# Attention scores of two heads on the two halves of the array's rows, with new tables of order and places, in a hybrid decoder layer

## The chip, the cores and the metric

The kernel runs on one core of a Trainium2 chip. The metric is the device time of one execution in microseconds; the time of a kernel is the median of its runs.

## The reference

One decoder layer for 512 tokens of width 1024, batch 1, float32 throughout. The input is normalised and multiplied by one wide matrix; its columns are the queries, keys and values of three attentions and three gates. The attentions are a sliding-window attention (8 query heads, 2 key heads of width 64, window 128, with a sink and a bias by distance), a stick-breaking attention (8 heads of width 64) and a cross-attention to 256 memory rows (4 heads of width 128). Each branch is projected, gated and added, then come an output matrix, a residual, and a SwiGLU network of width 2816.

```python
# sliding window, blocks of 128 queries against this block and the one before
scores = einsum('bnqhgd,bnkhd->bnhgqk', qb, kband) * d ** -0.5 + bias     # d = 64
# stick-breaking, block i of queries against all keys up to it
z = einsum('bqhd,bkhd->bhqk', q[:, i * 128:L], k[:, :L]) * d ** -0.5      # d = 64
log_1m = where(causal, log_sigmoid(-z), 0)
between = cumsum(log_1m, reverse) - log_1m
a = where(causal, exp(log_sigmoid(z) + between), 0)
out = einsum('bhqk,bkhd->bqhd', a, v[:, :L])
```

## The kernel before

**Precision.** A float32 factor x is kept as two parts in the type float32r: `hi`, a copy rounded on ScalarE, and `lo` = x - hi on VectorE (`split`, line 423). A product of two such factors is three matmuls into the same PSUM bank, hi*hi, hi*lo and lo*hi (`mm3`, line 455). Transposes and the products with the attention weights are in plain float32; one such matmul instruction appears in the trace as two passes.

**Units.** Most of the work is a stream of units (`Stream`, line 307): load a weight tile, split it, do its matmuls. `dn.run(us)` issues pieces of the stream worth that many microseconds by the units' own estimates. The attentions (`sb_head`, `swa_pair`, `mem_pair`) are issued between such pieces.

**Scores before.** A head is 64 wide, and the two heads of a pair lie on partitions 0-63 and 64-127 of one tile of 128 x 512. To fill the 128 rows of the array, `proj` (line 581) hands a finished block to one of two helpers, both of which work head by head on 64 partitions:

- `stack_parts` (line 553, for the stick-breaking keys `kb` and the sliding-window queries `qa`) puts hi on the head's own 64 partitions and lo on the other 64: one ScalarE copy and one VectorE subtraction a head.
- `stack_twice` (line 564, for the queries `qb` and the keys `ka`) puts hi on both halves, and lo on the head's half with zeros on the other: a GpSimd fill, a ScalarE copy, a VectorE subtraction and a VectorE copy a head.

There are 13 such blocks: four each of `kb`, `qb` and `qa`, and one `ka`. A head's score block is then two matmuls over all 128 rows: (hi, lo) against (hi, hi), and hi against lo with zeros. In `sb_head` (line 1273) a head has four query blocks with 512, 384, 256 and (two copies of 128, to fill the bank) 256 key columns, into three PSUM banks. In `swa_pair` (line 1348) a head has four query blocks of 256 columns each, into two banks.

**Around the scores.** After the scores of a head, ScalarE reads each bank twice (two sigmoids, into `br` and `bw`), VectorE masks and scans, `sb_turn` (line 1306) transposes the weights on TensorE (`c_ident`, `bw` in the trace), and `sb_out` (line 1323) multiplies them with the values: two heads on the two halves of the array's columns, 64 stationary columns each (`at`, `wide` in the trace, with the form 128x64). `swa_pair` ends in the same way (`pts`, `wide`). There are four calls of each.

**Order and places.** `ORDER` (line 38) holds one list for each engine: the order in which its instructions stand, counted as the program issues them; `Noted` (line 220) records them, and the end of the program (line 2095) chains them with dependencies that carry no semaphore. `PLAN` (line 148) names, for each buffer that is asked for, which place of its kind it gets: 8 PSUM banks, 73 tiles of 128 x 512 and others. Since every instruction goes through the recorder, nearly all lines of the trace are line 232.

Of the kernel before, what the change touches and what calls it, by code (L numbers as in the profile page):

```python
# [17 lines left out]
P = 128  # L18
# [19 lines left out]
ORDER = {  # L38
    "tensor": (
# [23 lines left out]
    ),  # L63
    "vector": (
# [81 lines left out]
    ),  # L146
}
PLAN = {
    "raw": (
# [2042 lines left out]
```

## Time and profile before

| | |
|---|---|
| median of 3 runs | 768.73 us (768.61 to 768.78) |
| span of the profiled execution | 766.9 us |
| TensorE matmuls / weight loads (busy) | 759.1 us, 4073 / 647.3 us, 4073 |
| VectorE, ScalarE, GpSimd (busy) | 675.2, 520.3, 104.1 us |
| DMA | 150.06 MB, mean 196 GB/s |
| stick-breaking: first score product / last product with the values start at | 81.5 us / 160.1 us |
| sliding window: first and last score product start at | 160.3 us / 211.7 us |

The profiled execution's own time is not listed apart from its span; the span runs from its first to its last instruction. Busy times of matmuls overlap (a matmul is counted until its last result is out), so what one costs in a row of them is read from one start to the next. PE is the matmul side of TensorE, PEld its weight loads.

### The profile page before, as it was taken

Reading aid. Unit: us, or ns where it says so; the run is one execution under the profiler, and the core shown is the slowest. Engines: PE = TensorE matmul, PEld = TensorE weight load, DVE = VectorE, ACT = ScalarE, POOL = GpSimd, SP = SyncE. Lnnn points to the kernel's source line nnn. Section 1 sums busy time; section 2 is a strip of 40 time slices with the busy share of each in tenths; the row PEclk is TensorE's granted clock in tenths of the full one; section 3 lists DMA queues with packets and bytes.
Section 4 is the critical chain, followed back from the end, with each engine's and each line's share of the span. In section 5 each row is a group of like instructions: output and inputs, shape, how many; then the busy total and the mean of one; then the engine's idle time right before and its main releaser. Section 6 shows DMA issues by size and latency. Waiting matters only on the chain.

```text
span 766.9 us, 11497 instructions
## 1 busy us (share of the span) xinstructions
PE 759.1 (99%) x4073; PEld 647.3 (84%) x4073; DVE 675.2 (88%) x1100; ACT 520.3 (68%) x946; POOL 104.1 (14%) x140
## 2 busy tenths in 40 slices
PE   9999999999999999999999999999999999999996
PEld 6789888778888888888888899988888888888885
DVE  7994897799989756999897799899999999999966
ACT  7662677777997758677944596566666668957552
POOL 0303242000222110010001201100000000214000
PEclk9999999999999999999999999999999999999998
DMA  8548999734799895469949958876777746859922
GB/s 277 166 142 233 332 328 254 211 111 149 185 188 192 184 203 163 112 134 210 340 128 329 209 130 240 203 191 180 204 192 203 220 142 187 171 120 216 261 75 111
DMA packets 50170, 150.06 MB, mean 196 GB/s; under 512 B 5984, under 2 KB 7952, under 8 KB 50016
## 3 DMA queue, kind: packets, MB, share of 16 engines
q1 hardware_dynamic: 34224, 94.38, 36.8%
q0 software_dynamic: 15600, 54.80, 36.1%
q8 instruction: 32, 0.52, 0.3%
q14 instruction: 26, 0.21, 0.1%
q10 hardware_dynamic: 288, 0.13, 0.1%
HBM read 140.38 MB, written 19.40 MB: 208 GB/s over the span
## 4 chain that ended last, share of the span: by engine, by line
PE 96%; DMA 1%; DVE 1%; ACT 1%; issue 0%; SPq 0%; DVEq 0%
PE bank L232 96%; DMA xT<-in_xT 1%; DMA raw<-in_w_p 0%; DVE xacc L232 0%; SPq L232 0%; ACT pair L232 0%; DVE pair L232 0%; ACT hi L232 0%; ACT xT L232 0%; DVE lo L232 0%; DVE fg L232 0%; DVE sl_x L232 0%; DVEq L2180 0%; DVE s L232 0%; ACT sqr L232 0%
## 5 line engine op out<-in xcount | busy, mean ns | idle before, releaser
L232 PE MATMUL bank<-pair,hi 128*128 128x512 f32 (+1 forms) x1008 | 254.4, 368 | 0.0
L232 DVE TENSOR_TENSOR lo<-raw,hi 128x1024 fp32r<-128x1024 f32 (+4 forms) x149 | 170.7, 1149 | 36.8 <-ACT hi L232 36.2
L232 PEld LDWEIGHTS bank<-pair,hi 128*128 128x128 f32 x1008 | 177.5, 189 | 27.0 <-ACT hi L232 0.9
L232 ACT CAST hi<-raw 128x1024 fp32r<-128x1024 f32 (+4 forms) x149 | 147.7, 998 | 73.7 <-PE bank L232 54.5
L232 PE MATMUL bank<-hi,pair 128*128 128x512 f32 (+1 forms) x628 | 196.3, 374 | 0.0
L232 PE MATMUL bank<-pair,lo 128*128 128x256 f32 (+1 forms) x752 | 154.7, 302 | 0.0
L232 PEld LDWEIGHTS bank<-hi,pair 128*128 128x128 f32 x628 | 115.3, 188 | 19.5 <-issue 0.2
L232 PEld LDWEIGHTS bank<-pair,lo 128*128 128x128 f32 x752 | 115.6, 190 | 10.9 <-DVE lo L232 0.7
L232 PE MATMUL bank<-lo,pair 128*128 128x512 f32 (+1 forms) x330 | 123.6, 375 | 0.0
L232 ACT CAST hi<-wide 128x1024 fp32r<-128x1024 f32 (+1 forms) x61 | 62.2, 1024 | 27.0 <-PE bank L232 11.3
L232 DVE TENSOR_TENSOR lo<-wide,hi 128x1024 fp32r<-128x1024 f32 (+1 forms) x61 | 71.9, 1185 | 4.6 <-ACT hi L232 4.3
L232 PEld LDWEIGHTS bank<-lo,pair 128*128 128x128 f32 x330 | 62.0, 188 | 10.1
L232 POOL DMA_DIRECT2D raw<-in_w_g x24 | 21.1, 878 | 124.4 <-DVE lo L232 106.2
L232 DVE TENSOR_TENSOR gp<-gp,bank 128x512 f32<-128x512 f32 x49 | 33.6, 687 | 4.6 <-PE bank L232 3.7
L232 ACT ACTIVATE sg<-gp 128x256 f32<-128x256 f32 x42 | 17.7, 421 | 23.0 <-DVE gp L232 22.9
L232 POOL DMA_DIRECT2D raw<-in_w_gu x15 | 13.2, 924 | 147.6 <-DMA raw<-in_w_gu 138.5
L232 ACT COPY gp<-bank 128x512 f32<-128x512 f32 x42 | 24.7, 588 | 2.1 <-DVE aq L232 1.4
L232 DVE TENSOR_TENSOR_SCAN bw<-br,bw 128x512 f32<-128x512 f32 (+3 forms) x32 | 24.6, 809 | 0.2
L232 DVE TENSOR_TENSOR gp<-gp,hp 128x512 f32<-128x512 f32 x36 | 24.7, 685 | 0.0
L232 POOL DMA_DIRECT2D wide<-in_w_gu x12 | 11.2, 934 | 84.6 <-DMA wide<-in_w_gu 76.3
L232 ACT COPY hp<-bank 128x512 f32<-128x512 f32 x36 | 21.5, 598 | 0.0
L232 PE MATMUL bank<-hi,ll 128*128 128x512 f32 x50 | 19.4, 389 | 0.0
(624 smaller groups left out, 1371.8 us busy)
## 6 DMA issues: line engine op xcount, KB each, us to landing
wide<-in_w_gu SPq DMA_DIRECT2D x31, 512.0 KB, 5.1
raw<-in_w_gu SPq DMA_DIRECT2D x26, 512.0 KB, 5.4
raw<-in_w_g POOLq DMA_DIRECT2D x24, 512.0 KB, 6.0
raw<-in_w_g SPq DMA_DIRECT2D x18, 512.0 KB, 4.2
raw<-in_w_gu POOLq DMA_DIRECT2D x15, 512.0 KB, 7.2
raw<-in_w_p SPq DMA_DIRECT2D x14, 512.0 KB, 6.3
wide<-in_w_gu POOLq DMA_DIRECT2D x12, 512.0 KB, 5.8
raw<-in_w_brt SPq DMA_DIRECT2D x9, 512.0 KB, 4.8
```

Of the source, the lines that this page charges most:

```text
L232: ins = f(*args, **kw)
```

## The change

Four things, of which the last touches every engine:

1. `stack_parts` and `stack_twice` go. `proj` splits each of the 13 blocks once, over all 128 partitions, with `parts` (one ScalarE copy, one VectorE subtraction).
2. Scores are made for two heads at once, each on its half of the array's rows. For every query block there is a run of six matmuls, hi*hi for both heads, lo*hi for both, hi*lo for both (`mm3_rows`), into different banks. A stick-breaking call (`sb_scores`, now for a pair of heads) has four such runs and fills six banks; a sliding-window call has four runs and fills four banks.
3. The loop over stick-breaking heads is one over pairs: the scores of pair c+1 are issued between the two `sb_turn` of pair c.
4. The program is first recorded as a list of operations, and then put out in one order over all engines (`ORDER` is now one list of 6346 numbers, from 0 to 6345, where it was five lists); `PLAN` is drawn up anew. Code for running without tables goes.

```diff
-                if kind in ("kb", "qa"):
-                    stack_parts(kind, idx, t)
-                elif kind in ("qb", "ka"):
-                    stack_twice(kind, idx, t)
-                elif kind == "qm":
-                    st[("qms", idx)] = parts(f"qms{idx}", t)
+                st[(kind + "s", idx)] = parts(f"{kind}s{idx}", t)
...
+    def mm3_rows(outs, l, r, start):
+        for x, y_ in ((0, 0), (1, 0), (0, 1)):
+            for e, out in enumerate(outs):
+                rows = slice(64 * e, 64 * e + 64)
+                mm(out, l[x][rows], r[y_][rows], start and x + y_ == 0, y_ == 1)
+
+    def sb_scores(c):
+        (kh, kl), (qh, ql) = st[("kbs", c)], st[("qbs", c)]
+        z = [[aps(f"z{2 * c + e}{i}") for i in range(3)] for e in range(2)]
         for r in range(NT):
...
-            mm(out, qs[:, q], keys, r < 3, False)
-            mm(out, ql[:, q], keys, False, r != 2)
+            mm3_rows([z[e][i][:, o : o + n] for e in range(2)], (qh[:, q], ql[:, q]), keys, r < 3)
+        for e in range(2):
+            sb_weights(2 * c + e, z[e])
...
     def swa_pair(c, bias):
...
-                mm(blocks(s[h], n), qs[:, q], kh, n in (0, 2), False)
-                mm(blocks(s[h], n), qs[:, q], klo, False, True)
+            mm3_rows([blocks(s[h], n) for h in hs], q, keys, n in (0, 2))
...
-    for h in range(8):
-        sb_head(h)
-        dn.run(3.0 if h < 2 else 2.6)
-        if h % 2 == 0 and h > 0:
-            sb_out(h // 2 - 1)
-        dn.run(3.0 if h < 2 else 2.6)
-        st.pop("turn")()
...
+    sb_scores(0)
+    dn.run(5.6)
+    for c in range(4):
+        sb_turn(2 * c)
+        dn.run(1.6)
...
+            sb_out(c - 1)
+        if c < 3:
+            sb_scores(c + 1)
+        dn.run(3.0)
+        sb_turn(2 * c + 1)
+        dn.run(6.4)
+    dn.run(1.0)
     sb_out(3)
```

Pieces of the new `ORDER`, in which a number is an operation of any engine. The first holds the score products of stick-breaking pair 0 (650 to 673; 700 and on are products of the stream), the second those of pair 1 (761 to 784), the third the second half of sliding-window pair 1 (1549 to 1560) behind column-half products of pair 0 (1525 to 1532):

```diff
+    "577 590 581 591-592 626 563 627 620 628-631 593 632 814 646 621 647-648 609 650-652 622 653-654 859 655-661 "
+    "637 700 639 638 701-702 817 703 640 704 649 705 641 706-707 642 662-664 643 665-667 708 674 709 644 675 710 "
+    "596 711 688 668 676 669-671 712 672 687 673 720-721 690 683 722 678 723-724 677 725-726 691 679 727 689 681 "
...
+    "749 685 747 623 750-751 686 752 742 692 753 698 746 743 645 744 754 745 755 697 756 818 815 761-763 811 "
+    "764-768 786 769 717 770-774 799 775-781 785 782-784 787 834 1071 699 837 798 839 819 794 820 789 821 801 "
...
+    "1562 1528 1631 1651 1529 1561 1530 1654 1577 1531-1532 1653 1578 1549-1550 1535 1551-1552 1762 1553-1554 "
+    "1536 1555-1556 1655 1557 1533 1558-1560 1594 1563 1595-1596 1534 1597 1786 1598 1580 1599 1564 1606 1600 "
```

More of the change, by code (lines that the diff above doesn't have):

```diff
@@ L1 @@
 import math
-from contextlib import ExitStack, nullcontext
+from contextlib import ExitStack
 import numpy as np
@@ L220 @@
-class Noted:
-    def __init__(self, engine):
-        self.engine, self.seen = engine, []
+ORDER = (
[257 rows of a table added]
+)
+PLAN = {
+    "raw": (
+        "0 1 2 3 0 1 2 3 0 1 2 3 0 1 0 2 3 1 0 2 3 1 2 3 2 0 3 2 3 0 1 0 2 1 3 0 2 3 1 0 2 3 2 3 2 3 1 0 1 0 1 0 2 3 "
+        "1 2 3 0 1 2 3 2 3 2 3 0 2 1 3 0"
+    ),
+    "hi": (
+        "0 1 2 3 1 2 0 3 1 2 3 0 1 0 3 2 1 0 3 2 1 0 3 2 3 0 2 0 2 3 1 0 2 1 3 2 0 1 3 2 0 1 3 2 0 1 3 2 0 1 2 3 0 1 "
+        "2 3 0 1 2 3 0 1 3 0 1 3 0 2 1 3 2 1 3 0 2 3 1 0 2 3 1 0 2 3 0 2 0 3 1 2 3 0 1 2"
+    ),
+    "lo": (
+        "0 1 2 3 2 1 0 3 2 1 3 0 2 1 3 0 1 2 0 3 1 2 0 3 0 2 3 0 3 2 1 0 3 2 1 2 3 2 1 3 0 3 1 2 0 3 1 2 0 3 2 1 3 0 "
+        "1 2 3 1 2 3 1 0 1 0 3 0 1 3 0 2 0 2 0 2 0 2 3 0 2 0 2 3 0 1 3 1 0 3 1 2 3 1 3 2"
+    ),
[21 rows of a table added]
+    ),
[5 rows of a table added]
+    ),
+    "s": (
+        "0 2 4 1 3 4 3 1 2 4 0 2 0 4 1 2 0 1 0 3 5 1 4 2 4 1 2 4 4 1 2 3 3 5 2 4 1 5 1 4 2 1 3 4 5 1 2 4 2 1 3 5 2 4 "
+        "3 5 1 4 1 5 3 6 2 5 0 6 3 5 3 0 6 2 6 2 5 1 0 11 10 8 3 10 8 9 7 9 8 10 4 10 8 9"
+    ),
+    "spare": (
+        "1 0 2 3 4 6 5 7 6 4 7 5"
+    ),
+    "fraw": (
+        "2 4 5 0 1 3 8 7 6 2 4 0 5 3 1 2 7 6 0 5 8 1 4 2 3 6 5 7 8 0 4 3 1 6 2 7 0 4 1 8 5 2 6 4 7 3 8 5 6 0 1 7 4 5 "
+        "2 3 6 0 8 4 1 2 5 3 6 7"
+    ),
+    "fhi": (
[3 rows of a table added]
+    ),
+    "flo": (
[3 rows of a table added]
+    ),
+    "ck2": (
+        "6 0 7 9 5 4 13 8 11 2 10 1 12 3"
+    ),
+    "p2": (
+        "2 1 3 0 1 2 2 1 0 1 0 2 0 3 1 3 0 1 0 1 3 3 0 0 1 0 3"
+    ),
+}
@@ new lines, with __init__, then, __getitem__ @@
+class View:
+    def __init__(self, make, path=(), shape=None):
+        self.make, self.path, self.shape = make, path, shape
+    def then(self, f):
+        return View(self.make, self.path + (f,))
+    def __getitem__(self, k):
+        return self.then(lambda ap: ap[k])
+    def bitcast(self, dt):
+        return self.then(lambda ap: ap.bitcast(dt))
+    def rearrange(self, *args, **kw):
+        return self.then(lambda ap: ap.rearrange(*args, **kw))
+    def unsqueeze(self, axis):
+        return self.then(lambda ap: ap.unsqueeze(axis))
+    def to_broadcast(self, shape):
+        return self.then(lambda ap: ap.to_broadcast(shape))
+    def real(self):
+        ap = self.make()
+        for f in self.path:
+            ap = f(ap)
+        return ap
@@ new lines, with __init__, put_out @@
+class Op:
+    def __init__(self, at, engine, name, args, kw):
+        self.at, self.engine, self.name, self.args, self.kw = at, engine, name, args, kw
+        self.behind = ()
+class Program:
+    def __init__(self):
+        self.ops = []
+    def put_out(self, nc, order, follow):
+        real = lambda x: x.real() if isinstance(x, View) else x
+        last, out = {}, set()
+        for n in order or range(len(self.ops)):
+            op = self.ops[n]
+            assert all(b.at in out for b in op.behind)
+            out.add(n)
+            args = [real(x) for x in op.args]
+            ins = getattr(getattr(nc, op.engine), op.name)(*args, **{k: real(x) for k, x in op.kw.items()})
+            if op.engine in last:
+                follow(ins, last[op.engine])
+            last[op.engine] = ins
+        assert len(out) == len(self.ops)
@@ L256, in __getitem__, with once, f @@
         return self.held[c]
+def once(make):
+    got = []
+    def f():
+        if not got:
+            got.append(make())
+        return got[0]
+    return f
 class Places:
@@ L268, in open, with fixed, take @@
     def open(self, pool, kind, n, shape, dt=F32):
-        for i in range(n if PLAN else 0):
+        for i in range(n):
             key = f"{kind}{i}"
             self.held[key] = pool.tile(shape, dt, tag=key, name=key, bufs=1)
-    def fixed(self, pool, shape, dt, name):
-        if not PLAN:
-            return pool.tile(shape, dt, name=name)
+    def fixed(self, shape, name):
         if name == "v_all":
             self.spare = self.used
-        n = shape[1] if dt == F32 else shape[1] // 2
-        t = self.held["wide0"][:, self.used : self.used + n]
-        self.used += n
-        return t if dt == F32 else t.bitcast(dt)
-    def take(self, pool, kind, shape, dt, name, **kw):
-        if kind not in PLAN:
-            return pool.tile(shape, dt, tag="ck" if kind == "spare" else kind, name=name, **kw)
+        t = self.held["wide0"][:, self.used : self.used + shape[1]]
+        self.used += shape[1]
+        return t
+    def take(self, pool, kind, shape, dt, name):
         n = int(next(self.plan[kind]))
         if kind == "ck" and n < SINGLES:
-            return pool.tile(shape, dt, tag=f"ck{n}", name=name, bufs=1)
+            return View(once(lambda: pool.tile(shape, dt, tag=f"ck{n}", name=name, bufs=1)))
         if kind == "ck":
+            assert dt == F32R
             n -= SINGLES
@@ L412, in dps @@
     def dps(name):
-        return places.take(psd, "p" if PLAN else "d", [P, 512], F32, name)
+        return places.take(psa, "p", [P, 512], F32, name)
     def aps(name):
-        return places.take(psa, "p" if PLAN else "a", [P, 512], F32, name)
+        return places.take(psa, "p", [P, 512], F32, name)
     def banks(name):
@@ L425, in split @@
         ins = nc.scalar.copy(hi, raw)
[L426 to L429 removed]
+        nc.vector.tensor_tensor(lo, raw, hi.bitcast(F32), op=ALU.subtract)
         return ins
@@ L441, in w_split @@
         uid[0] += 1
-        hi = places.take(wp, "hi", [P, 1024], F32R, f"hi{uid[0]}", bufs=4)
-        lo = places.take(wp, "lo", [P, 1024], F32R, f"lo{uid[0]}", bufs=4)
+        hi = places.take(wp, "hi", [P, 1024], F32R, f"hi{uid[0]}")
+        lo = places.take(wp, "lo", [P, 1024], F32R, f"lo{uid[0]}")
         if isinstance(raw, list):
             for i, x in enumerate(raw):
-                ins = split(x[:, :], hi[:, i * 512 : (i + 1) * 512], lo[:, i * 512 : (i + 1) * 512])
+                split(x[:, :], hi[:, i * 512 : (i + 1) * 512], lo[:, i * 512 : (i + 1) * 512])
         else:
-            ins = split(raw[:, :n], hi[:, :n], lo[:, :n])
-        if "chain" in st:
-            after(ins, st["chain"])
+            split(raw[:, :n], hi[:, :n], lo[:, :n])
         return hi, lo
@@ L456, in mm3 @@
         (lh, ll), (rh, rl) = l, r
-        one = nc.tensor.matmul(out, lh, rh, start=start, stop=False, skip_group_check=True)
+        nc.tensor.matmul(out, lh, rh, start=start, stop=False, skip_group_check=True)
         nc.tensor.matmul(out, lh, rl, start=False, stop=False, skip_group_check=True)
-        return one, nc.tensor.matmul(out, ll, rh, start=False, stop=stop, skip_group_check=True)
-    def mm3_behind(*args):
-        one, last = mm3(*args)
-        if "products" in st:
-            after(one, st["products"])
-        st["products"] = last
+        nc.tensor.matmul(out, ll, rh, start=False, stop=stop, skip_group_check=True)
     def mm(out, l, r, start, stop):
@@ L474, in tile_kernel @@
     pin, since = [], []
-    def after(ins, first):
-        if not ORDER:
-            follow(ins, first)
     def follow(ins, first):
@@ L486, in fn @@
         ins = nc.scalar.activation(*args, **kw)
-        for p in pin:
-            after(ins, p)
+        ins.behind = tuple(pin)
         since.append(ins)
@@ L494, in table, with const @@
         ins = nc.scalar.preload_act_table_set(name)
-        for x in since:
-            after(ins, x)
+        ins.behind = tuple(since)
         since.clear()
         pin[:] = [ins]
-    def const(name, shape, pool=cst):
-        t = places.fixed(cst, shape, F32, f"c_{name}") if pool is cst else pool.tile(shape, F32, name=f"c_{name}")
+    def const(name, shape, pool=None):
+        t = pool.tile(shape, F32, name=f"c_{name}") if pool else places.fixed(shape, f"c_{name}")
         nc.sync.dma_start(t[:, :], a[name])
@@ L862, in gen @@
                 for k in range(2):
-                    mm3_behind(qbank[key][:, :], q_left(p, c, k, i), cols((hi, lo), k * 512, 512), first and k == 0, c == 1 and k == 1)
+                    mm3(qbank[key][:, :], q_left(p, c, k, i), cols((hi, lo), k * 512, 512), first and k == 0, c == 1 and k == 1)
                 yield 1.36
@@ L971, in gen @@
                 for k in range(2):
-                    mm3_behind(sbank[i][:, :], seven_left(b, p, k, i), cols((hi, lo), k * 512, 512), first and k == 0, last and k == 1)
+                    mm3(sbank[i][:, :], seven_left(b, p, k, i), cols((hi, lo), k * 512, 512), first and k == 0, last and k == 1)
                 yield 1.36
@@ L1143, in tile_kernel @@
     raws = [places.take(wp, "raw", [P, 1024], F32, f"raw_first{i}") for i in range(FIRST)]
-    his = [places.take(wp, "hi", [P, 1024], F32R, f"hi_first{i}", bufs=4) for i in range(FIRST)]
-    los = [places.take(wp, "lo", [P, 1024], F32R, f"lo_first{i}", bufs=4) for i in range(FIRST)]
+    his = [places.take(wp, "hi", [P, 1024], F32R, f"hi_first{i}") for i in range(FIRST)]
+    los = [places.take(wp, "lo", [P, 1024], F32R, f"lo_first{i}") for i in range(FIRST)]
     def first_load(eng, p, units=range(FIRST)):
@@ L1210, in tile_kernel @@
-    pin[:] = [first_table]
+    idle = tc.nc.const_aps.tensor(1.0, [P, 512], BF16)
+    one_t = {}
+    for name in ("x", "m"):
+        one_t[name] = ck(f"on_{name}", F32R)[:, :P]
+        nc.vector.tensor_copy(one_t[name], idle[:, :P])
+    pw = dps("warm")
+    for i in range(WARM):
+        mm(pw[:, :], idle[:, :P], idle[:, :], True, True)
+    first_load(nc.scalar, 0, (0, 2))
+    first_table = nc.scalar.preload_act_table_set("natural_log_exp_and_others")
+    pin[:] = [first_table]
+    load_x(0, 1)
@@ new lines, in tile_kernel @@
+    first_load(nc.sync, 0, (1,))
+    load_x(1, 2)
+    first_load(nc.sync, 1, (0, 1))
+    load_x(2, 3)
+    first_load(nc.sync, 1, (2,))
+    first_load(nc.sync, 2, (0,))
+    load_x(3, 4)
+    first_load(nc.sync, 2, (1, 2))
+    load_x(4, 5)
+    first_load(nc.sync, 3)
+    load_x(5, 8)
+    dn.loaded = dn.have = FIRST
+    for p in range(len(PIECE)):
+        for i in range(FIRST):
+            first_split(i, p)
+        for k in range(*PIECE[p]):
+            gain_split(k)
+    xacc = ck("xacc")
@@ new lines, in tile_kernel @@
+    nc.scalar.activation(xacc[:, :], xraw[0][:, :], AF.Square)
+    for k in range(1, KC):
+        nc.scalar.activation(xraw[k][:, :], xraw[k][:, :], AF.Square)
+        nc.vector.tensor_tensor(xacc[:, :], xacc[:, :], xraw[k][:, :], op=ALU.add)
+    dn.ahead(4, 3)
+    for i in range(FIRST):
+        first_ps[("kb", i)] = aps(f"kb{i}")
+    order = [(i, 0, x) for x in ("hh", "lh", "hl") for i in range(FIRST)]
+    order += [(i, 1, x) for i in range(FIRST) for x in ("hh", "lh", "hl")]
+    for i, k, x in order:
+        w = (his if x[0] == "h" else los)[i]
+        mm(first_ps[("kb", i)][:, :], w[:, k * P : (k + 1) * P], u[k][x[1] == "l"], k == 0 and x == "hh", False)
@@ L1212, in tile_kernel @@
+    gens = [dn.units[i]["mm"](his[i], los[i]) for i in range(FIRST)]
+    for k in range(2, KC + 1):
+        for g in gens:
+            next(g, None)
+    dn.at = FIRST
+    st["rs"], st["rb"] = rstd_of("x", xacc, S, aps)
+    for f in st.pop("waiting"):
+        f()
     ident = const("ident", [P, P], base)
-    sinks = places.fixed(cst, [P, 8], F32, "sinks")
+    sinks = places.fixed([P, 8], "sinks")
     nc.sync.dma_start(sinks[:, :], a["sinks"].to_broadcast([P, 8]))
@@ L1271, in pair_out @@
                 seven_sums(b)
-    def sb_head(h):
-        c = h // 2
-        ks, qs, ql = (st[(x, c, h % 2)] for x in ("kbs", "qbs", "qbl"))
-        z = [aps(f"z{h}{i}") for i in range(3)]
+    def mm3_rows(outs, l, r, start):
[6 more added lines that the diff above has]
+        z = [[aps(f"z{2 * c + e}{i}") for i in range(3)] for e in range(2)]
         for r in range(NT):
@@ L1620, in turn @@
         st[("t1", t)] = t1
-        return place("T1", t, t1)
+        place("T1", t, t1)
     def kept(t):
@@ L1985, in tile_kernel @@
     dn.until(f"branch{MEM}")
-    if PLAN:
-        fp = None
-    else:
-        first.close()
-        fp = ctx.enter_context(tc.tile_pool(name="fp", bufs=9, reuse_waits="tile"))
+    fp = wp
     def f_split(raw, n):
         uid[0] += 1
-        hi = places.take(fp, "fhi", [P, 1024], F32R, f"hi{uid[0]}", bufs=4)
-        lo = places.take(fp, "flo", [P, 1024], F32R, f"lo{uid[0]}", bufs=4)
+        hi = places.take(fp, "fhi", [P, 1024], F32R, f"hi{uid[0]}")
+        lo = places.take(fp, "flo", [P, 1024], F32R, f"lo{uid[0]}")
         if isinstance(raw, list):
@@ L2065, in tile_kernel @@
     kept(1)
-    behind(since[-1], st["mixed"])
     table("silu_and_others")
@@ L2071, in tile_kernel @@
     go(3)
-    behind(*turn(3, tmp[3]))
+    turn(3, tmp[3])
     fs.hold = 5
@@ L2075, in tile_kernel @@
     turn_n2(2)
-    behind(*turn_n2(3))
+    turn_n2(3)
     fs.hold = 6
@@ L2079, in tile_kernel @@
     turn_n22(2)
-    behind(*turn_n22(3))
+    turn_n22(3)
     fs.hold = 8
@@ L2083, in tile_kernel @@
     for t in (2, 3):
-        late = turn_late(t, 0)
-    behind(*late)
+        turn_late(t, 0)
     fs.hold = 10
@@ L2089, in tile_kernel @@
         turn_late(t, 1)
-    st.pop("behind")
     fs.hold = 10**6
@@ L2094, in tile_kernel @@
     go(len(fs.units))
-    for e, text in ORDER.items():
-        seen, last = getattr(nc, e).seen, None
-        for part in text.split():
-            a, _, b = part.partition("-")
-            for k in range(int(a), int(b or a) + 1):
-                if last is not None:
-                    follow(seen[k], seen[last])
-                last = k
+    order = []
+    for part in ORDER.split():
+        a, _, b = part.partition("-")
+        order += range(int(a), int(b or a) + 1)
+    program.put_out(tc.nc, order, follow)
 def _buckets():
```

289 lines of the change are left out of this document (71 added, 218 removed), and 413 rows, old and new, of tables (ORDER, PLAN).

## The prediction

> **What bounds the kernel now.** I read the page first, then the waits of TensorE, then the matmuls in order of time around the scores.
>
> ```profile
> span 766.9 us, 11497 instructions
> PE 759.1 (99%) x4073; PEld 647.3 (84%) x4073; DVE 675.2 (88%) x1100; ACT 520.3 (68%) x946; POOL 104.1 (14%) x140
> PE   9999999999999999999999999999999999999996
> PE 96%; DMA 1%; DVE 1%; ACT 1%; issue 0%; SPq 0%; DVEq 0%
> PE bank L232 <- PEq L2174: 0.8, 1, 0.8
> PE bank L232 <- DVE sl_x L232: 0.4, 1, 0.4
> ```
>
> TensorE is busy in every slice, it makes 96% of the chain that ended last, and the two rows of its waits, the whole answer, add up to 1.2 us. So an edit is worth what it does to the stream of matmuls; work saved on VectorE, ScalarE and GpSimd is worth nothing while that stream doesn't wait for it. The sum below is therefore a sum over TensorE alone. The profiled execution spans 766.9 us and the median of the runs is 768.73, so 1.8 us lie around the span; I keep them.
>
> **What a score product costs now.** One head of stick-breaking, in order of time (start, duration; durations overlap, so the cost is from start to start):
>
> ```profile
> 81.53 0.40 PE L232 MATMUL bank<-kbs,qbs 128*128 128x512 f32 x1
> 81.76 0.39 PE L232 MATMUL bank<-kbs,pair 128*128 128x512 f32 x1
> ...
> 82.82 0.63 PE L232 MATMUL bank<-pair,hi 128*128 128x512 f32 x2
> ...
> 177.28 0.28 PE L232 MATMUL bank<-kal,qas 128*128 128x256 f32 x1
> 177.40 0.28 PE L232 MATMUL bank<-pair,qas 128*128 128x256 f32 x1
> ```
>
> Eight products, two each of 512 and 384 columns and four of 256, go from 81.53 to 82.82: 1.29 us a head, 0.23 of it for one of 512. A sliding-window product, of 256 columns, is 0.12 us.
>
> **The change, part by part.** *Products.* Per pair of heads and query block there were four products on all rows (two a head); now there are six on half the rows, two at a time if the halves run side by side, so three places instead of four. Stick-breaking: 4 pairs x 2 x 1.29 = 10.3 us becomes 7.7, saved 2.6. Sliding window: 16 runs x 4 x 0.12 = 7.7 us becomes 5.8, saved 1.9. Together **-4.5 us**. No row shows row halves; the nearest are the column halves of `sb_out`, which this kernel has already:
>
> ```profile
> 107.94 0.71 PE L232 MATMUL bank<-c_ident,bw 128*128 128x128 f32 x5
> 108.40 0.36 PE L232 MATMUL bank<-kbs,qbs 128*128 128x256 f32 x1
> 108.61 0.28 PE L232 MATMUL bank<-kbs,qbl 128*128 128x256 f32 x1
> ...
> 108.85 0.28 PE L232 MATMUL bank<-kbs,qbl 128*128 128x256 f32 x1
> 109.05 1.08 PE L232 MATMUL bank<-at,wide 128*64 128x512 f32 x4
> ...
> 111.36 0.39 PE L232 MATMUL bank<-mh,hi 128*128 128x256 f32 x1
> 111.58 0.28 PE L232 MATMUL bank<-ml,hi 128*128 128x256 f32 x1
> ...
> L232 PEld LDWEIGHTS bank<-at,wide x64: 132/137/137, 109.1 to 160.0; 128*64 128x64 f32 x64
> 109.54 0.14 PEld L232 LDWEIGHTS bank<-at,wide 128*64 128x64 f32 x2 [0.29 <-DVE wide L232]
> 109.97 0.14 PEld L232 LDWEIGHTS bank<-at,wide 128*64 128x64 f32 x2 [0.29 <-issue]
> ...
> 111.47 0.19 PEld L232 LDWEIGHTS bank<-ml,hi 128*128 128x128 f32 x1
> ```
>
> Five full-width float32 transposes and one 256-column product go from 107.94 to 108.61, 0.67 us; less 0.12, a 128-column float32 pass takes 0.11. One `sb_out` is 16 matmuls (two heads, four key blocks, two passes each) of 2 x 2 x (512+384+256+128) = 5120 columns: one after the other 40 x 0.11 = 4.4 us. It takes 109.05 to 111.36 = 2.31 us: the halves do run side by side. So do their loads: two in 0.14 us, where one takes 0.137. I take the same for row halves. The price of a place could differ: a pass of 512 float32 columns takes 0.43 us here (109.54 to 109.97), 0.215 for each of two goes, and a 512-column product of the scores 0.23, so about 0.01 us of each is a gap that the column halves do not show. Without it the 96 new places (48 in each attention) cost 1 us less, with it twice 1 us more: ends -5.5 and -3.5.
>
> *Changes between full array and halves.* This speaks against the change. Before the column halves the last full product holds 0.20 us (108.85 to 109.05) instead of 0.12: 0.08 of waiting. Then their first load is not hidden: 0.05 us. After them: 2.31 us are 0.16 more than the 2.15 that 1280 columns a pass, two passes, take at 0.43 for 512; 0.05 of it is that load, 0.10 a second wait; and the next full product holds 0.22 (111.36 to 111.58) instead of 0.12, its own load laid open. A 64-column load is 0.14 and a 128-column one 0.19, so 64 columns take 0.05 and 128 take 0.10. So: into column halves 0.14, out to the full array 0.20, and row halves, whose stationary operand has 128 columns, by estimate 0.20 in (bounds: 0, if rows need no change, and 0.20). The Trainium skill, "TensorEngine Tiling (Array Packing)", Key Properties, says that changing the tiling mode drains TensorE, while a change of tile within a mode does not. The trace agrees for column halves (0.20 against 0.12); for row halves no run here shows it. By that rule the sum is the one below; without it, rival C.
>
> How many changes? I numbered the operations of the new code in the order in which it issues them (unit by unit, with the microseconds of each `dn.run`), and looked them up in the new `ORDER`. The 24 products of each call are 650-673, 761-784, 943-966 and 1138-1161 (stick-breaking), 1387-1410, 1537-1560, 1700-1723 and 1873-1896 (sliding window). The runs of six stay whole. Stick-breaking pair 0 comes in three pieces with full products between, pairs 1 and 2 in one each, pair 3 in two, the first straight before `sb_out(1)`. Sliding-window pair 0 stands straight behind `sb_out(3)`, pair 2 straight before the column halves of pair 1, pairs 1 and 3 in two pieces around the column halves of the pair before. That makes 35 changes of form, where the eight calls with column halves made 16 before. Of the 35, eight go into column halves and 27 into row halves or the full array: 8 x 0.14 + 27 x 0.20 = 6.5 us. Before: 8 x 0.14 + 8 x 0.20 = 2.7. Together **+3.8 us**.
>
> *Splits.* Of 13 key and query blocks, 26 half-height copies on ScalarE become 13 whole ones, 36 VectorE instructions 13, ten GpSimd fills go.
>
> ```profile
> L232 ACT CAST qbs<-qb x5: 617/619/622, 35.1 to 46.5; 64x512 fp32r<-64x512 f32 x5
> L232 DVE CAST qbs<-qb x5: 421/423/424, 36.8 to 48.3; 64x512 fp32r<-64x512 f32 x5
> L232 DVE TENSOR_TENSOR kbs<-kb,kbs x5: 683/685/687, 32.3 to 48.6; 64x512 fp32r<-64x512 f32 x5
> L232 POOL MEMSET qbl<- x5: 522/522/527, 22.9 to 26.2; 64x512 f32 x5
> L232 DVE TENSOR_TENSOR sl_x<-xacc,sh_x x1: 684/684/684, 21.6 to 21.6; 128x512 fp32r<-128x512 f32 x1
> 759.86 0.39 PE L232 MATMUL bank<-hi,pair 128*128 128x512 f32 x1
> ```
>
> A half-height instruction costs what a whole one does (685 ns on 64 partitions, 684 on 128), so ScalarE is freed of 13 x 0.62 = 8 us, VectorE of 13 x 0.69 + 10 x 0.42 = 13 us, GpSimd of 10 x 0.52 = 5 us, from 22 to 160 us of the span. All of it lies beside matmuls that don't wait (the two waits above): 0, at best the 0.4 us at `sl_x`.
>
> *Tables.* `PLAN` and `ORDER` are new for the whole kernel: every engine's order, SP's and GpSimd's DMA issues among it, and every buffer. What they can win is bounded by the waits above, 0.4 us (the 0.8 is the start). What they can lose has no row. The last 40 matmuls, the stores and the VectorE steps behind them come in nearly the old order, so the tail after the last matmul (759.86 in the rows just shown, to 766.9) stays. I take 0, with -0.4 and +3 as ends.
>
> Sum: -4.5 + 3.8 = -0.7 us: 766.9 becomes 766.2, and with the 1.8 around it **768.0**.
>
> **Rivals.** *A, rows do not run side by side.* Six places instead of three or four: 10.3 x 6/4 + 7.7 x 6/4 - 18.0 = +9.0, with the 3.8: 781.5. Against it stands the pair of column halves in the time of one. In the Trainium skill, "TensorE: Matmul & The Clock Gate", Part 3, four 32-row tiles measured 3.07 times faster; no run here shows that yet.
>
> *B, side by side, but the two loads of a place one after the other.* A place is then no shorter than 2 x 0.10: sliding window 48 x 0.21 = 10.1 instead of 7.7, stick-breaking 4 x (3 x 0.23 + 9 x 0.21) = 10.3, no change; +2.4 + 3.8 = +6.2, 774.9. Against it: two column loads in the time of one.
>
> *C, row halves need no wait and hide their loads.* Then only the column changes of today are paid: 768.7 - 4.5 = 764.2. For it: nothing in the trace has half rows. If half of the wait and load is hidden, 766.1.
>
> *D, the slower side: the banks.* A call of `sb_scores` now fills six of PSUM's eight banks at once, where a head filled three.
>
> ```profile
> L232 ACT ACTIVATE br<-bank x24: 485/530/630, 83.3 to 148.9; 128x384 f32<-128x384 f32 x16, 128x512 f32<-128x512 f32 x8
> L232 ACT ACTIVATE bw<-bank x24: 486/560/642, 84.2 to 149.6; 128x384 f32<-128x384 f32 x16, 128x512 f32<-128x512 f32 x8
> 80.00:120.00 40.00, 40.00 (x262) 35.45 (x261) 35.55 (x60) 29.14 (x56) 13.38 (x21) 1.00 1.02 320
> ```
>
> Each bank is read twice by ScalarE, so a pair takes 12 x 0.55 = 6.5 us to free, during which the stream has two banks. ScalarE has room there (29 of 40 us), but DMA is full in that stretch (share 1.02), so a load that a new order issues later is not caught up. If each of the four calls makes TensorE wait 0.9 us, the sum is +2.9: 771.6. It decides from 2.2 us of waits in all. Against it: pair 0 comes in three pieces, the others with neighbours from both sides, as if banks were reckoned with.
>
> **How the numbers follow.** Forecast 0.45 with its own range 767.2 to 770.3 (place prices half way to their ends, -5.0 to -4.0, tables -0.3 to +1.8); C 0.18; D 0.16; A 0.05; B 0.06; the remaining 0.10 is the forecast with the cheaper place (-5.5) and the best tables, 766.6 to 767.1. A measurement of this kernel tells about 0.2% from no change, 1.5 us. Faster than 767.2: C and that last case, with a little of the forecast's edge, 0.31. Slower than 770.3: A, B and most of D, 0.24. Within: 0.45. The range that leaves out A, B and the far ends of C and D is 764.2 to 771.2.
>
> **What would show it.** Right: in the timeline, two half-row products start within 0.01 us of each other and the pair takes 0.23 or 0.12; the product before a run holds 0.08 longer than usual, and the first load of a run is open; TensorE still has no wait above 1 us; 4137 matmuls. Rows one after the other, or pairs 0.21 apart at 256 columns, would be A or B; no gap at the ends of runs, C; rows in the waits of TensorE for ScalarE or VectorE between 80 and 160 us, D. A wait of TensorE for DMA or splits outside the attention stretch would be the tables, and would make the prediction wrong for a reason that has nothing to do with the halves.

## The result: 1.7% slower, and the profile after

The changed kernel takes 781.68 us (median of 4 runs, 780.66 to 782.46) beside 768.75 us for the kernel before on the same chip; the ratio is 1.0169, with a 95% interval of 1.0155 to 1.0183. The forecast was 768.0 with a range of 764.2 to 771.2. The time happens to be that of rival A, but rival A did not happen.

First the head of the page after, the row of the slices of TensorE, and the shares of the chain of work that ended last:

```profile
span 780.7 us, 11677 instructions
PE 765.8 (98%) x4137; PEld 639.0 (82%) x4137; DVE 657.6 (84%) x1077; ACT 512.7 (66%) x934; POOL 102.3 (13%) x130
PE   9999999999999999999999999999999999999995
PE 78%; ACT 9%; DMA 6%; DVE 5%; issue 2%; SPq 0%; DVEq 0%; ACTq 0%; POOLq 0%
```

TensorE still looks busy in nearly every slice, because each matmul is counted until its last result is out. The chain shows the difference: TensorE made 96% of it before, now 78%, and ScalarE, DMA and VectorE 20%. ScalarE and VectorE do 8 and 18 us less work (8 and 13 were worked out for the splits), and the kernel is slower all the same.

The waits of TensorE (engine, released by: us in total, times, longest) had two rows before; now they have twelve, of which these are the first five:

```profile
PE bank L419 <- ACT gq1p L419: 1.7, 3, 1.1
PE bank L419 <- PEq L2287: 0.8, 1, 0.8
PE bank L419 <- ACT gq0p L419: 0.7, 1, 0.7
PE bank L419 <- ACT hi L419: 0.7, 1, 0.7
PE bank L419 <- DVE pair L419: 0.6, 2, 0.4
...
```

The first and third rows are copies of gate sums (`gq`), far behind the attention scores.

The halves themselves did what was forecast. This is the timeline of the first run of scores (start, duration, tiles; `x2` is a pair), matmuls and then their weight loads:

```profile
81.03 0.39 PE L419 MATMUL bank<-pair,lo 128*128 128x512 f32 x1
81.35 0.50 PE L419 MATMUL bank<-kbs0h,qbs0h 64*128 64x512 f32 x2
81.69 0.40 PE L419 MATMUL bank<-kbs0h,qbs0l 64*128 64x512 f32 x2
81.92 0.40 PE L419 MATMUL bank<-kbs0l,qbs0h 64*128 64x512 f32 x2
...
81.35 0.18 PEld L419 LDWEIGHTS bank<-kbs0h,qbs0h 64*128 64x128 f32 x2 [0.35 <-issue]
81.46 0.19 PEld L419 LDWEIGHTS bank<-kbs0h,qbs0l 64*128 64x128 f32 x2
```

Two products of 512 columns take 0.23 us together (81.69 to 81.92); within a pair the starts are 3 ns apart (in 77 of the 96 pairs 3 or 4 ns, at most 10). So they run side by side, and so do their loads. The product before the run holds 0.32 us (81.03 to 81.35) instead of 0.23: 0.09 of waiting. The first pair holds 0.34 instead of 0.23: its load is open.

**Where the time went.** Every kernel here issues the same 3881 matmul instructions that are not scores (each is one instruction of the program; of the float32 ones the products with the attention weights have two rows in the trace, and a transpose, other than said above, has one: 80 rows for the 80 transposes of the stick-breaking weights). I counted them in order of their starts and noted by how much the k-th one is later than in the kernel before (us; "loads free" and "old order" are experiments below):

| k-th product | starts before at | changed kernel | loads free | old order |
|---|---|---|---|---|
| 405 (ahead of the scores) | 80.1 | -0.2 | 0.0 | -0.2 |
| 786 (stick-breaking done) | 160.0 | +0.5 | +0.6 | -0.4 |
| 1061 (sliding window done) | 224.1 | +2.1 | +2.3 | +0.9 |
| 1406 | 300.0 | +6.0 | +3.1 | +0.9 |
| 1882 (gates done) | 400.2 | +9.5 | +5.1 | +0.9 |
| 3441 (gate and up products done) | 660.1 | +12.0 | +7.5 | +0.9 |
| last | 759.9 | +12.3 | +7.8 | +0.9 |
| end of the span | 766.9 | +13.8 | +9.3 | +0.9 |

The attention stretch, where the halves are, costs 2.1 us. The gate stage behind it costs 7.4, the feed-forward stage 2.5, the tail behind the last matmul 1.5. In those three nothing but the tables was changed.

Two windows show what the tables moved (window, its length, busy us and counts of PE, PEld, DVE, ACT, POOL, clock, DMA share, GB/s): first two of the kernel before, then the same two after.

```profile
120.00:160.00 40.00, 40.00 (x218) 30.77 (x218) 32.67 (x50) 29.79 (x58) 4.83 (x7) 1.00 0.79 224
...
280.00:300.00 20.00, 20.00 (x99) 16.89 (x98) 13.86 (x17) 12.80 (x17) 0.00 (x0) 1.00 0.68 192
```

```profile
120.00:160.00 40.00, 39.85 (x228) 30.79 (x227) 25.25 (x36) 23.76 (x42) 3.44 (x5) 1.00 0.45 152
...
280.00:300.00 20.00, 20.00 (x89) 16.32 (x88) 11.41 (x12) 11.77 (x17) 3.96 (x5) 1.00 1.01 245
```

DMA work has left the stretch from 120 to 160 us (share 0.79 to 0.45) for the gate stage (0.68 to 1.01 from 280). Part of it are the sums of branch weights (`w_sum`: GpSimd issues a copy of 512 KB from DRAM to DRAM and an accumulation onto it, four pairs for each of two branches). The tile `ws2p` in the trace of before, then of after:

```profile
L232 POOL DMA_DIRECT2D ws2p<-in_w_brt x6: 517/812/1454, 64.6 to 131.7; - x6
```

```profile
L419 POOL DMA_DIRECT2D ws2p<-in_w_brt x6: 813/835/1194, 246.3 to 297.3; - x6
```

Issued from 64.6 to 131.7 us before, from 246.3 to 297.3 now, between the gate loads that GpSimd also issues. Of those, the pages before and after have the first two of these rows among their DMA issues (count, KB each, median us from issue to landing), and the waits after have the third (us in total, times, longest):

```profile
raw<-in_w_g POOLq DMA_DIRECT2D x24, 512.0 KB, 6.0
```

```profile
raw<-in_w_g POOLq DMA_DIRECT2D x24, 512.0 KB, 7.7
```

```profile
ACT hi L419 <- DMA raw<-in_w_g: 16.0, 9, 4.0
```

A gate load that GpSimd issues takes 7.7 us (6.0 before), and ScalarE's splits wait 16.0 us for gate weights, a row that the waits of before did not have. One instance, in the timeline after, on GpSimd, ScalarE and TensorE:

```profile
245.73 0.87 POOL L419 DMA_DIRECT2D raw<-in_w_g  x1 [4.42 <-ACT hi L419]
246.28 0.87 POOL L419 DMA_DIRECT2D ws2p<-in_w_brt  x1
256.48 1.35 POOL L419 DMA_DIRECT2D ws2p<-in_w_brt  x2 [9.33 <-DMA ws2p<-in_w_brt]
...
254.33 1.05 ACT L419 CAST hi<-raw 128x1024 fp32r<-128x1024 f32 x1 [2.18 <-DMA raw<-in_w_g]
255.29 0.71 ACT L419 ACTIVATE gq1p<-gq1p,wide 128x512 f32<-128x512 f32 x1
255.91 0.56 ACT L419 COPY gq1p<-bank 128x512 f32<-128x512 f32 x1
...
255.05 0.39 PE L419 MATMUL bank<-hi,pair 128*128 128x512 f32 x1
256.52 0.73 PE L419 MATMUL bank<-hi,pair 128*128 128x512 f32 x2 [1.09 <-ACT gq1p L419]
```

The load is issued at 245.73 and the split that needs it starts at 254.33, after 2.18 us of waiting; behind the split stand a sigmoid and the copy that frees a PSUM bank; TensorE, which needs that bank, starts its next matmul 1.5 us after the one at 255.05; in an unbroken row it is 0.23. Two steps off, a transfer moved by the table stops the bounding engine.

### The profile page after: what moved, and what is told of

Its sections match the earlier page's. It is cut to its first block, busy times and chain, and to the rows that moved or that the text cites. A ratio compares the mean times of both kernels' runs of the same rounds, so it can differ in the third digit from the quotient of the medians.

```text
span 780.7 us, 11677 instructions
## 1 busy us (share of the span) xinstructions
PE 765.8 (98%) x4137; PEld 639.0 (82%) x4137; DVE 657.6 (84%) x1077; ACT 512.7 (66%) x934; POOL 102.3 (13%) x130
## 4 chain that ended last, share of the span: by engine, by line
PE 78%; ACT 9%; DMA 6%; DVE 5%; issue 2%; SPq 0%; DVEq 0%; ACTq 0%; POOLq 0%
PE bank L419 78%; DMA raw<-in_w_g 3%; ACT hi L419 2%; DMA raw<-in_w_brt 2%; DVE lo L419 1%; ACT pair L419 1%; DVE pair L419 1%; ACT gq1p L419 1%; DMA xT<-in_xT 1%; DVE s L419 1%; ACT gq2p L419 1%; ACT bw L419 1%; ACT br L419 1%; ACT w L419 0%; DVE wide L419 0%
## 5 line engine op out<-in xcount | busy, mean ns | idle before, releaser
L419 PE MATMUL bank<-pair,hi 128*128 128x512 f32 (+1 forms) x1064 | 269.8, 366 | 1.5 <-ACT hi L419 0.7
L419 PE MATMUL bank<-hi,pair 128*128 128x512 f32 (+1 forms) x784 | 239.3, 380 | 2.3 <-ACT gq1p L419 1.3
L419 ACT CAST hi<-raw 128x1024 fp32r<-128x1024 f32 (+5 forms) x150 | 148.6, 996 | 96.8 <-PE bank L419 59.7
L419 DVE TENSOR_TENSOR lo<-raw,hi 128x1024 fp32r<-128x1024 f32 (+5 forms) x150 | 171.4, 1148 | 35.4 <-ACT hi L419 27.1
L419 PEld LDWEIGHTS bank<-hi,pair 128*128 128x128 f32 x784 | 144.4, 188 | 32.8 <-ACT gq1p L419 2.4
L419 PE MATMUL bank<-pair,lo 128*128 128x256 f32 (+1 forms) x784 | 166.6, 302 | 0.0
L419 PE MATMUL bank<-lo,pair 128*128 128x512 f32 (+1 forms) x390 | 144.7, 379 | 0.0
L419 PEld LDWEIGHTS bank<-lo,pair 128*128 128x128 f32 x390 | 73.1, 188 | 12.7 <-DVE lo L419 0.7
L419 PE MATMUL bank<-pair,pair 128*128 128x512 f32 (+4 forms) x151 | 37.0, 367 | 0.0
L419 PEld LDWEIGHTS bank<-pair,pair 128*128 128x128 f32 (+1 forms) x151 | 23.9, 187 | 4.9 <-issue 0.5
```

The lines of the kernel that those rows point to most:

```text
L419: ins = getattr(getattr(nc, op.engine), op.name)(*args, **{k: real(x) for k, x in op.kw.items()})
```

## The experiments

Theory 1: the new tables cost the time, by transfers that moved into the gate stage. Theory 2: the new tables cost it, by the order of ScalarE and VectorE. Theory 3: the halves cost more than reckoned. (The kernel before ran beside each experiment, at 768.5 to 768.7 us.)

### Sums early, and splits that wait for no load

The first edit: behind operation 618, the last bias load, go the sixteen transfers of the branch sums.

```diff
+    early = [1074, 863, 1075, 892, 1091, 893, 1092, 999, 1121, 1000, 1122, 1029, 1200, 1030, 1201]
+    order = [n for n in order if n not in early and n != 862]
+    at = order.index(618) + 1
+    order[at:at] = [862] + early
```

> The changed kernel, with the sixteen GpSimd transfers that build the sums of branch weights (512 KB each, DRAM to DRAM) put back to back behind the last bias load, at about 125 us, instead of 125.7 to 297.3 us. Theory 1 (the new tables moved transfers out of the attention stage into the gate stage, where gate weights now land late): 3 to 5 us faster than the changed kernel, 777 to 779 us, and TensorE's waits for ScalarE between 240 and 300 us shrink. Theory 2 (the new order of ScalarE and VectorE itself, not the transfers): within 0.5 us of 781.7. Theory 3 (the halves cost more than reckoned): within 0.5 us of 781.7.

Measured: **779.65 us** (779.23 to 779.95), 2.0 us faster than the changed kernel, less than the 3 to 5 that theory 1 gave and more than the 0.5 of the others. ScalarE's wait for gate weights falls from 16.0 to 6.2 us:

```profile
ACT hi L419 <- DMA raw<-in_w_g: 6.2, 5, 2.0
```

The second edit, in the split of a weight block; the units of the gates and of the summed branch weights set `free`:

```diff
+        elif "free" in st:
+            x = ident[:, :].unsqueeze(1).to_broadcast([P, 8, P])
+            three = lambda t: t[:, :n].rearrange("p (a b) -> p a b", a=8)
+            split(x, three(hi), three(lo))
```

> The changed kernel, with the splits of the gate weights and of the summed branch weights of the sliding window and the memory reading a resident constant tile instead of the loaded weights, so that they never wait for a load; all loads are still made (the weights' values are left out). Theory 1 (late loads): 5 to 7 us faster than the changed kernel, 775 to 777 us. Theory 2 (engine order): about 1 us faster. Theory 3 (halves): no change, 781 to 782 us.

Measured: **778.12 us** (777.48 to 778.74), 3.6 us faster by the medians, 4.5 by the spans (776.2 for 780.7). The table above has it as "loads free": of the 7.4 us that the gate stage costs, 2.8 stay. So late loads are real and are worth about 4 us, less than I expected, and they are not all of it. The four runs of the changed kernel also lie further apart than those of the kernel before (1.8 us from lowest to highest, against 0.4).

### The halves undone under the new tables

An operation whose name is `None` is not put out:

```diff
-                rows = slice(64 * e, 64 * e + 64)
-                mm(out, l[x][rows], r[y_][rows], start and x + y_ == 0, y_ == 1)
+                one = mm(out, l[x], r[y_], start and x + y_ == 0, y_ == 1)
+                if x == 1:
+                    one.name = None
```

> The changed kernel, its tables as they are, but the scores in two products of all 128 rows for each head and block as before instead of three of half the rows: no changes of form to and from row halves, the places of before (the third product is left out, and both heads' rows are summed, so the values are not those of the reference). Theories 1 and 2 (the tables): the places give 4.4 us back and the changes 3.6 us, so 780 to 784 us. Theory 3 (the halves cost it): 768 to 771 us.

Measured: **785.01 us** (783.52 to 787.38), 1 us above what theories 1 and 2 gave. Without the halves the changed kernel is 3.3 us slower, not faster. Theory 3 falls. The 3.3 us are not the worth of the halves alone: counted as in the table above, the 1061st product starts 2.76 us late here and 2.13 in the changed kernel, so in the stretch where they stand the halves gain 0.63 us by these two traces. The rest of the distance comes up behind it, in work that is the same in both.

### The changes of form by themselves

The kernel before with its own tables; each score product reads only the 64 rows of its head (`swa_pair` is changed in the same way):

```diff
-            mm(out, qs[:, q], keys, r < 3, False)
-            mm(out, ql[:, q], keys, False, r != 2)
+            rows = slice(64 * (h % 2), 64 * (h % 2) + 64)
+            mm(out, qs[rows, q], keys[rows], r < 3, False)
+            mm(out, ql[rows, q], keys[rows], False, r != 2)
```

> The kernel before with its own tables, and each score product on the 64 rows of its head instead of all 128 (half of each stacked sum is left out): the same number of products at the same places, one after the other, with the changes of form to and from row halves, about 32 of them. By the price of the prediction (0.1 to 0.2 us a change): 772 to 775 us. If row halves need no wait: 768 to 769 us. Theory 3 (halves cost much more than reckoned, by banks or by the products): 778 us or more.

Measured: **774.47 us** (774.4 to 774.53), +5.75. In its trace the form changes 54 times where it changed 16 times before, so 0.15 us a change. The entry looks as it did in the pairs: 0.21 us for a product of 0.12 ahead of it, 0.34 for the first one of 0.23.

```profile
106.55 0.28 PE L232 MATMUL bank<-mh,lo 128*128 128x256 f32 x1
106.76 0.49 PE L232 MATMUL bank<-kbs,qbs 64*128 64x512 f32 x1
107.10 0.39 PE L232 MATMUL bank<-kbs,qbl 64*128 64x512 f32 x1
```

### The tail

Read in order of time, ScalarE's square of the last bank and VectorE's product from the same bank, in the kernel before (last matmul at 759.86) and after (772.16):

```profile
760.29 0.60 ACT L232 ACTIVATE sqr<-bank 128x512 f32<-128x512 f32 x1 [2.15 <-PE bank L232]
...
761.08 0.68 DVE L232 TENSOR_TENSOR fg<-bank,bc_g_fpost 128x512 f32<-128x512 f32 x1
```

```profile
772.10 1.41 DVE L419 SCALAR_TENSOR_TENSOR fg<-fg,s,hr 128x512 f32<-128x512 f32 x2
773.43 0.68 DVE L419 TENSOR_TENSOR fg<-bank,bc_g_fpost 128x512 f32<-128x512 f32 x1
...
774.15 0.60 ACT L419 ACTIVATE sqr<-bank 128x512 f32<-128x512 f32 x1 [2.53 <-DVE fg L419]
```

The two readers of one bank run one after the other, in the order in which the table names them. Before, ScalarE was first and started 0.43 us after the last matmul. Now VectorE is first, and it has 1.41 us of the piece before it to do; ScalarE starts 1.99 us after the last matmul. The edit, on top of the early sums:

```diff
+    for product, behind in ((6314, 6310), (6341, 6337)):
+        order.remove(product)
+        order.insert(order.index(behind) + 1, product)
```

> The kernel of the early sums (779.65 us), and in the last two pieces of the down projection VectorE's product with the gain is put behind ScalarE's square of the same bank, as the kernel before has it; the new tables put it ahead. Theory: after the last matmul ScalarE waits for that product, which waits for the output of the piece before; the time from the last matmul's start to the end falls from 8.5 to 7.1 us, and the time to 778.2 us. If the tail has another cause: no change of it, 779 to 780 us.

Measured: **778.14 us** (777.45 to 780.0), 1.5 faster than with the early sums alone, and 7.07 us from the last matmul to the end, as before.

### The halves in the old order

To test all tables at once I gave the changed code the old ones: I sorted its operations by the time at which each started in the profiled execution of the kernel before, and kept the old places. Only the scores of the second head of each pair go forward to the first's, with banks chosen anew for them.

> The code of the changed kernel (scores on row halves, blocks split once) with tables that repeat the kernel before: every operation stands in the order in which it started in the profiled execution of the kernel before, in the same places; only the scores of the second head of each pair move forward to those of the first, in one run a pair, with banks chosen anew between 64 and 190 us. Theory 1 and 2 (the new tables cost the time): the places give 4.4 us, eight runs cost about 0.3 us each for their changes: 766 to 768.5 us, at or below the kernel before. Theory 3 (the halves cost it, through banks or changes): 775 us or more.

Measured: **771.46 us** (771.17 to 771.8), 10.2 us below the changed kernel with the same code. Theory 3's 775 is excluded once more, but the 766 to 768.5 is missed. (In this order one weight split stands ahead of three products that should read the tile's old contents, so those read other values; the work is the same, and in the later versions it stands behind them.) Three waits of 0.5 us or more are new. All three stand in the attention stretch (at 109, 199 and 203 us), where moved scores brought TensorE early to work that another engine does at its old time:

```profile
PE bank L398 <- DVE wide L398: 1.3, 1, 1.3
PE bank L398 <- ACT sp L398: 1.0, 1, 1.0
...
PE bank L398 <- DVE lo L398: 0.5, 1, 0.5
...
```

> The kernel with the halves in the old order, with its scores in two products of all 128 rows again (the third product is left out and both heads' rows are summed, so the values are not the reference's): as the kernel before but for the place of the second head's scores, the banks and the splits. All theories: 768 to 770 us; its distance to the kernel with halves in the old order is the net worth of the halves, which the changed kernel showed as 3.3 us. More than 772 us would mean that the moved scores or the banks cost by themselves.

Measured: **773.14 us** (772.77 to 773.18). So the halves gain 1.7 us in the old order. What this version shares with the halves, the moved scores with their banks and the splits, costs 4.5 us beside the kernel before; these were not tried apart. The distance of 3.3 was not repeated. Next I moved what those waits stood in front of:

> The halves in the old order (771.46 us) with three moves in its tables: the first stick-breaking output stands 1.5 us later, since TensorE, which the moved scores brought there earlier, waited 1.3 us for VectorE's value steps; the scores of the last sliding-window pair run in two stretches, its first two blocks at 196.6 us and the others behind the output of the pair before, where TensorE had waited 1.0 and 0.5 us. Theory (the tables decide; the halves gain 1.7 us net at this count of runs): those waits go, 768 to 769.5 us. If the waits only move on: 770.5 to 772 us.

Measured: **773.55 us** (773.32 to 773.8), 2.1 us slower. I had added 1.5 us to the start of each product of the first output, and so mixed its eight products with others:

```profile
109.74 1.08 PE L398 MATMUL bank<-at,wide 128*64 128x512 f32 x4 [1.30 <-DVE wide L398]
110.75 0.38 PE L398 MATMUL bank<-mh,hi 128*128 128x256 f32 x1
111.06 0.86 PE L398 MATMUL bank<-at,wide 128*64 128x384 f32 x2
111.85 0.39 PE L398 MATMUL bank<-ml,hi 128*128 128x256 f32 x1
```

Instead of two changes of form the first output now makes fourteen (42 for 29 in the whole kernel), and 3.05 us more are lost between 100 and 120 us: 0.25 us for each of the twelve, and the wait was still there. (Lost is the time from a matmul's start to the next, less what such a matmul takes in an unbroken row: 0.227 us for 512 columns, 0.171 for 384, 0.117 for 256, half of it for row halves.) Put as blocks:

> The halves in the old order, mended: the run before had the eight products of the first stick-breaking output mixed with other products in seven stretches (42 changes of form for 29, 3.05 us more lost between 100 and 120 us) and did not delay its first one. Here the output stands as one block behind the next 3.6 us of other work, the third output stands directly behind the scores of the last stick-breaking pair, and the last sliding-window pair keeps its two stretches; 29 changes of form. Theory (the tables decide): the 3.05 us and the 1.3 us wait go, 768.5 to 770 us. If TensorE is then only early for the next work: 771 us.

Measured: **769.6 us** (769.09 to 770.18); ratio to the kernel before 1.0014, interval 1.0005 to 1.0023. It is "old order" in the table of lags: 0.9 us late when the attentions are done, and not a tenth more in the 540 us behind them. The waits of TensorE are five rows again, the last two of 0.2 us; the first three:

```profile
PE bank L397 <- PEq L2265: 0.8, 1, 0.8
PE bank L397 <- ACT bs L397: 0.6, 1, 0.6
PE bank L397 <- ACT hi L397: 0.4, 1, 0.4
...
```

No version beat the kernel before.

### Late sums in the old order, and all splits free

The second of the three versions above (773.55 us), with the sixteen sums put between the same GpSimd neighbours as in the changed kernel:

> The same, but the sixteen GpSimd transfers of the branch sums take the places in the GpSimd queue that the changed kernel gives them (behind the last bias load and between the gate loads) instead of those of the old order. Theory 1 (late transfers cost the gate stage): 2 to 4 us slower than the same kernel with the sums early, 770 to 773 us, with waits of TensorE for ScalarE's splits between 240 and 300 us. Theory 2 (only the order of ScalarE and VectorE counts): within 0.5 us of it.

Measured: **801.9 us** (797.74 to 804.46), 28 us slower than that version, ten times what I expected. Here it is not the gate weights that come late but the sums of input quarters that GpSimd issues in the same queue (`xq<-xq`). Its timeline on GpSimd and VectorE, and the longest wait of TensorE:

```profile
210.90 1.47 POOL L397 DMA_DIRECT2D ws0p<-in_w_brt  x1
220.91 0.52 POOL L397 DMA_DIRECT2D ws0p<-ws0p  x1 [8.54 <-DMA ws0p<-in_w_brt]
...
239.00 0.81 POOL L397 DMA_DIRECT2D ws0p<-in_w_brt  x1 [4.44 <-DMA ws0p<-ws0p]
239.53 2.11 POOL L397 DMA_DIRECT2D xq<-xq  x2
...
248.64 0.56 DVE L397 COPY pts<-bank 128x384 f32<-128x384 f32 x1 [21.11 <-DMA xq<-xq]
```

```profile
PE bank L397 <- DVE pts L397: 19.8, 1, 19.8
```

The chain of branch sums, each of which waits for the one before, holds GpSimd's queue from 210.9 to 239.0 us. The `xq` sum behind it is issued 28 us late. `pts`, a copy out of PSUM that has nothing to do with either, is planned into a tile that this sum must read first, and TensorE waits for `pts`. The wait is not all of the 28 us: this trace grants TensorE half its clock (0.5) from 231.7 to 255.6 us and from 303.4 to 306.8 us, and products of 512 columns start 0.43 us apart there instead of 0.23, about 4 us in all. So a late transfer does cost time, here by another way than in the gate stage; its price depends on what stands behind it.

> The changed kernel with the order of its last two VectorE products as before (1.5 us, shown), and every split of a weight block after the first fourteen reading a resident constant instead of the loaded block, in the attention, gate and feed-forward stages (the weights' values are left out; all loads are made). If the late loads that cost time are those of the gate stage (3.5 us, shown) and the rest of the tables' 12 us is the order of ScalarE, VectorE and TensorE: 776 to 777 us. If loads are late elsewhere too: 770 to 774 us, near the halves in the old order.

Measured: **777.77 us** (777.57 to 780.01), 0.8 us above the upper end of the first case and 3.8 above that of the second. Loads are not late anywhere else in a way that counts: up to 660 us its lags are those of the second experiment within 0.2 us, and the tail's 1.5 us is lost again to two new waits in the down projection (it comes 0.5 and 0.7 us later by them). So what is left of the gate stage and the feed-forward stage, 2.8 and 2.5 us, is no wait of a split for its load.

**The account of the 13.8 us** by spans: attentions 2.1; gate stage 7.4, of it 4.6 by splits that wait for loads (shown by freeing them) and 2.8 that stay when no split waits for its load; feed-forward stage 2.5 in some thirty gaps of less than 0.5 us; last stretch 0.3; tail 1.5 (shown by the order). The 2.13 of the attentions are 2.76 with whole rows and the same tables, less the 0.63 that the halves gain there. That the old tables do away with all of it behind the attentions is shown. Which pairs of instructions in the two stages make the 2.8 and the 2.5 was not tried one by one, nor the order apart from the places, and both stay open.

## Why the prediction was wrong

The step that failed is *Tables*: "I take 0, with -0.4 and +3 as ends". It was worth about 12 us: the same code took 781.7 with the new tables and 769.6 with the old. The upper end had no row behind it ("What they can lose has no row"), and I took that for a small number. But there were rows to be bounded by. `ORDER` moves every DMA issue, and before the change DMA was full or nearly so in stretch after stretch, as this row of its page shows (tenths of the 16 DMA engines' time in 40 slices):

```profile
DMA  8548999734799895469949958876777746859922
```

A list of transfers that pass from one stage to another can be read out of `ORDER` before the run, as I did for the scores alone. That "TensorE still has no wait above 1 us" failed with it (1.1 us).

- **Tail.** "The tail ... stays" because the last steps "come in nearly the old order". Nearly was the fault: one VectorE product had passed ScalarE's square of the same bank, 1.45 us.
- **Products.** -4.5 us held: beside the same tables with whole rows the halves gain 0.6 us and lose 3.75 on changes of form, so the places give 4.4. Pairs run side by side (0.23 us for two of 512 columns), and so do their loads.
- **Changes.** 0.20 us into rows held to the hundredth in the first run (0.09 of waiting, 0.11 of open load). The changed kernel has 34 changes where I counted 35. Without its row halves it loses 3.75 us less between 80 and 220 us, over 18 changes: the term was +3.8. By themselves 38 more changes cost 5.75 us. The rule of the Trainium skill, "TensorEngine Tiling (Array Packing)", Key Properties, that a change of mode drains TensorE, agrees for rows as well: the last full product holds 0.32 us for 0.23. Rival C is out.
- **The sum of the halves**, -0.7 us, held under the new tables: 0.6 us by the traces, in the stretch where they stand. In the old order they gain 1.7 us with 13 changes more where the changed kernel has 18. The whole change in the old order, mended, is at +1.1 us: what the halves gain goes into scores that moved, with waits where TensorE came early.
- **Splits** at 0: 8 us less on ScalarE and 18 on VectorE bought nothing that any run shows; no run has the splits alone.
- **Rivals.** A and B did not happen. D's place was wrong: none of the larger waits lies at the six banks.
- The sign that would tell ("a wait of TensorE for DMA or splits outside the attention stretch would be the tables") was named, and it is what the profile shows. It was priced at 0 with +3 us as its upper end and given no rival of its own.

## What to carry to other kernels

When a change draws up a whole schedule anew, the schedule is the change: list which transfers pass from one stage into another and which instruction of another engine now stands ahead of a bounding engine's release, and bound that cost by what is queued behind each, not by the waits of the kernel before. To judge an edit apart from its schedule, put its operations into the order of the old trace; here that turned 12.9 us into 1.1. And a gain on the bounding engine is a gain only if the engines that feed it can be early too.

## What was not expected of the hardware

- Two engines that read the same PSUM bank ran one after the other in the tails shown (0.60 and 0.68 us), so that the order in the table decides who waits: the trace has VectorE's product as what releases ScalarE's square. The Trainium skill, "PSUM — Partial Sum Buffer", section "PSUM bank collisions raise a hardware error", states that two engines may not be on one bank and quadrant at once, reads against reads included; the trace agrees in that these two never overlap.
- A chain of transfers in GpSimd's queue held TensorE for 19.8 us, over a sum that it did not need and the reuse of one tile. In that trace the granted clock was 0.5 during most of the wait and for 6 us behind it.
